# Moving 32 modulation slots from two feed-forward stages into two token mixers

## The chip, the cores and the metric

The kernel runs on one core of a Trainium2 chip. The metric is the device time of one launch in microseconds (us). Five engines work side by side, each through its own instructions in a fixed order: TensorE (PE, matmuls; PEld is its weight load), VectorE (DVE), ScalarE (ACT), GpSimd (POOL) and SyncE (SP, which here only issues DMAs). They wait for each other by semaphores.

## The reference, cut to what matters

Three transformer blocks run one after the other on 512 latent tokens (and 256 context tokens) of width 1024, all in float32. Each block starts from six modulation vectors per stream, computed from a conditioning vector alone, and not from the tokens:

```
m = jnp.dot(jax.nn.silu(cond), w_mod) + b_mod        # w_mod: 1024 x 6144
sh1, sc1, g1, sh2, sc2, g2 = split(m, 6)

h = rms_norm(x, norm1_g) * (1 + sc1) + sh1            # mixer
q, k, v, u_pool, a, b = split(h @ w_in)
attn = differential attention over latent and context tokens, 4 heads
mix  = concat(attn, pool_mixer(u_pool), conformer_conv(a, b))
x = x + g1 * (mix @ w_out)

h2 = rms_norm(x, norm2_g) * (1 + sc2) + sh2           # feed-forward (FFN)
x = x + g2 * ((silu(h2 @ w_g) * (h2 @ w_u)) @ w_down) # hidden width 2816
```

Blocks 0 and 1 have this form; in block 0 the context tokens go through the same steps. Block 2 has another mixer (latent attention and a gated recurrence) and the same kind of FFN. So the modulation of a block only has to be ready before that block uses it, and may be computed at any earlier time.

## The kernel before, in words

**Matmuls.** Weights and activations are split into a high and a low part (tiles `whi`/`wlo`, `hh`/`hl`, `gh`/`gl`), and every product is three matmuls (`mm3`, L255, L258, L259). A weight comes as two half tiles `raw` of 512 KB by SP's DMA queue (L227); ACT copies it to `whi` (L230), and POOL subtracts to get `wlo` (L231). Weights are loaded one ahead (`Weights.next`), `whi`/`wlo` have two buffers, and `raw` has four, taken in turn.

**Modulation slots.** The three blocks' modulation is cut into 72 slots of 256 columns (24 for each block). One slot, `mod_slot`, loads two `raw` halves (1 MB, L219, from the same four buffers and the same SP queue as the weights; the next slot's load is put in ahead of it), runs 8 small matmuls on PE (L344; the trace has two records of each), copies the result by ACT (`ev`, L350), transposes it with two PE matmuls (L355), and reduces, adds and scales on DVE (L357, L359, L363). The PSUM tiles of a slot carry a tag: `"pj"` in the mixers (the same two buffers that the projections of q, v and the pool use), `"ap"` in the FFNs, where no other matmul of that part uses it.

**Stages.** `start` runs 8 slots with the first norm. `layer(l)` is the mixer of block l: for each head there is a list of items (`windows`) that is issued step by step between the attention's steps. An item is a projection of the next head (`q`, `v`), four taps of the depthwise convolution (`t`; L666 on DVE, L671 on ACT, L672 on POOL), the pooling mixer, the convolution's layer norm, half of the output projection (`o`), or a modulation slot (`m`). `MODS_MIX[l]` gives the number of slots in the lists of heads 0 to 3. Attention runs at a raised priority, the taps at a lowered one. `ffn(l)` goes through 22 steps j of 128 hidden columns, with 48 matmuls on 512 latent columns each (and 48 on 256 context columns in block 0), and issues `MODS_FFN[l][j]` slots behind step j; after some steps a part of the down projection follows.

**Order.** The program's order is not the engines' order: a scheduler with its own estimate of durations and the priorities above sets, for each engine, what stands behind what. Once built, each engine's list is fixed, and an engine whose next instruction waits does nothing else.

Of the kernel before, what the change touches and what calls it, by code (L numbers as in the profile page):

```python
# [24 lines left out]
NJ = FF // 128  # L25
# [217 lines left out]
class K:  # L243
# [472 lines left out]
        return post(g, ps)  # L716


    MODS_MIX = [(4, 8, 0, 0), (2, 4, 2, 0)]
    MODS_FFN = [[1] * NJ, [1] * NJ, [0] * NJ]  # L720

    LAST = [(0, 0, 0.2, 0.4, 0.6, 0.8, 1), (0, 0.1, 0.4, 0.7, 1)]
    SLOT = {"g": 0, "u": 1, "p": 2, "v0": 3, "q0": 4, "q1": 5, "v1": 6, "q2": 7, "q3": 8}
# [1 line left out]
    def windows(self, l):  # L725
# [22 lines left out]
        q0, v0 = tm("q0"), tm("v0")  # L748
        nm = self.MODS_MIX[l]
        conv = [it for g in ("01", "2") for n in "gu" for it in fm(n) if it[2] in g]  # L750
# [175 lines left out]
    def ffn(self, l, pf, hx, hc, xt, xc, then, at=None):  # L926
# [5 lines left out]
        for gi, (j0, jn, cn) in enumerate(DOWN[l]):  # L932
            gt = []
            for j in range(j0, j0 + jn):
# [28 lines left out]
                gt.append((gh, gl))  # L963
                self.mod_fill(self.MODS_FFN[l][j], "ap", j == j0 + jn - 1)
                if at and j in at:
# [783 lines left out]
```

## Time and profile before

| | before |
|---|---|
| median of 3 runs | 2667.38 us (2660.89 to 2668.7) |
| profiled execution | 2666.06 us, of which the trace spans 2664.3 us |
| PE busy | 2516.9 us, 94% of the span |
| POOL, ACT, DVE busy | 1250.2, 959.7, 951.1 us |
| granted PE clock, mean | 0.966 |

The stages in the trace, read from where their tiles begin and end: start 0 to 104 us, mixer 0 from 104 (with its output projection to 479), FFN 0 from 479 to 1067, mixer 1 from 1067 to 1412 (its output projection from about 1349), FFN 1 from 1412 to 1827, block 2 from 1827 to the end. A row of a table of stretches gives each engine's busy time in it, the granted PE clock as a share of full speed, the DMA engines' busy share and GB/s. Busy time cannot tell a matmul at half clock from one at full clock, so both columns are read together.

### The profile page before, as it was taken

Reading aid. Unit: us, or ns where it says so; the run is one execution under the profiler, and the core shown is the slowest. Engines: PE = TensorE matmul, PEld = TensorE weight load, DVE = VectorE, ACT = ScalarE, POOL = GpSimd, SP = SyncE. Lnnn points to the kernel's source line nnn. Section 1 sums busy time; section 2 is a strip of 40 time slices with the busy share of each in tenths; the row PEclk is TensorE's granted clock in tenths of the full one; section 3 lists DMA queues with packets and bytes.
Section 4 is the critical chain, followed back from the end, with each engine's and each line's share of the span. In section 5 each row is a group of like instructions: output and inputs, shape, how many; then the busy total and the mean of one; then the engine's idle time right before and its main releaser. Section 6 shows DMA issues by size and latency. Waiting matters only on the chain.

```text
span 2664.3 us, 38718 instructions
## 1 busy us (share of the span) xinstructions
PE 2516.9 (94%) x15840; PEld 2143.2 (80%) x15840; DVE 951.1 (36%) x1864; ACT 959.7 (36%) x1973; POOL 1250.2 (47%) x1033
## 2 busy tenths in 40 slices
PE   7889979999999999999889999999998899999998
PEld 5767869988888889877788777778887788888887
DVE  4787463221120223479443111114321756210112
ACT  4454453412212123354434223224443543422222
POOL 4886323533333334688326445545322344555553
PEclk9889989999999999989989999999998899999999
DMA  7113311323223223222223434343101021223221
GB/s 251 48 48 96 127 71 33 111 85 121 87 94 104 95 96 100 78 64 80 90 85 115 162 121 161 123 154 115 64 32 50 16 87 56 80 95 95 94 89 55
DMA packets 68964, 248.57 MB, mean 93 GB/s; under 512 B 7473, under 2 KB 10801, under 8 KB 67121
## 3 DMA queue, kind: packets, MB, share of 16 engines
q1 hardware_dynamic: 64992, 231.11, 26.6%
q10 hardware_dynamic: 3792, 14.97, 1.5%
q8 instruction: 125, 2.05, 0.3%
q14 instruction: 55, 0.44, 0.1%
HBM read 239.75 MB, written 6.29 MB: 92 GB/s over the span
## 4 chain that ended last, share of the span: by engine, by line
PE 46%; DVE 6%; ACT 2%; POOL 2%; DMA 1%; issue 1%; POOLq 0%; DVEq 0%; ACTq 0%
PE s2t L259 6%; PE s2t L258 6%; PE s2t L255 6%; PE pj L255 5%; PE pj L258 5%; PE pj L259 5%; PE ap L829 1%; PE ap L258 1%; PE ap L259 1%; PE ap L255 1%; POOL wlo L231 1%; PE s2t L1535 1%; PE s2t L846 1%; DVE mix L666 1%; PE ap L344 1%
## 5 line engine op out<-in xcount | busy, mean ns | idle before, releaser
L231 POOL TENSOR_TENSOR wlo<-raw,whi 128x512 fp32r<-128x512 f32 x576 | 743.5, 1321 | 681.6 <-ACT whi L230 681.2
L230 ACT CAST whi<-raw 128x512 fp32r<-128x512 f32 x576 | 319.5, 616 | 670.0 <-PE pj L258 244.7
L255 PE MATMUL s2t<-hh,whi 128*128 128x512 f32 (+1 forms) x1184 | 445.8, 377 | 2.3 <-ACT whi L230 2.3
L259 PE MATMUL s2t<-hh,wlo 128*128 128x512 f32 (+1 forms) x1184 | 447.8, 378 | 0.0
L258 PE MATMUL s2t<-hl,whi 128*128 128x512 f32 (+1 forms) x1184 | 445.8, 377 | 0.8 <-POOL hl L429 0.8
L255 PE MATMUL pj<-hh,whi 128*128 128x256 f32 (+1 forms) x1088 | 336.8, 311 | 11.0 <-DVE mod L357 4.3
L258 PE MATMUL pj<-hl,whi 128*128 128x256 f32 (+1 forms) x1088 | 331.6, 305 | 2.1 <-POOL hl L429 1.1
L259 PE MATMUL pj<-hh,wlo 128*128 128x256 f32 (+1 forms) x1088 | 331.6, 306 | 0.3 <-POOL wlo L231 0.3
L959 DVE TENSOR_TENSOR sg<-sg,s2t 128x512 f32<-128x512 f32 x66 | 45.4, 688 | 652.9 <-ACT sg L958 652.9
L255 PEld LDWEIGHTS s2t<-hh,whi 128*128 128x128 f32 x1184 | 222.0, 188 | 48.3 <-ACT whi L230 3.0
L258 PEld LDWEIGHTS s2t<-hl,whi 128*128 128x128 f32 x1184 | 222.2, 188 | 46.7 <-POOL hl L429 1.5
L259 PEld LDWEIGHTS s2t<-hh,wlo 128*128 128x128 f32 x1184 | 222.5, 188 | 44.6 <-issue 1.2
L328 POOL TENSOR_TENSOR gl<-sg,gh 128x512 fp32r<-128x512 f32 (+1 forms) x66 | 97.5, 1478 | 289.1 <-ACT gh L327 289.0
L255 PEld LDWEIGHTS pj<-hh,whi 128*128 128x128 f32 x1088 | 210.0, 194 | 27.8 <-DVE mod L357 4.6
L258 PEld LDWEIGHTS pj<-hl,whi 128*128 128x128 f32 x1088 | 210.5, 193 | 11.4 <-POOL hl L429 1.4
L259 PEld LDWEIGHTS pj<-hh,wlo 128*128 128x128 f32 x1088 | 209.9, 193 | 8.8 <-POOL wlo L231 0.5
L255 PE MATMUL pj<-whi,hh 128*128 128x256 f32 x672 | 196.8, 293 | 0.9 <-ACT v L709 0.9
L258 PE MATMUL pj<-wlo,hh 128*128 128x256 f32 x672 | 196.2, 292 | 0.0
L259 PE MATMUL pj<-whi,hl 128*128 128x256 f32 x672 | 194.7, 290 | 0.0
L898 DVE SCALAR_TENSOR_TENSOR xt<-pj,mod,xt 128x256 f32<-128x256 f32 x224 | 101.7, 480 | 177.7 <-PE pj L259 176.6
L958 ACT ACTIVATE sg<-s2t 128x512 f32<-128x512 f32 x66 | 39.2, 594 | 303.8 <-PE s2t L259 303.8
L259 PE MATMUL pj<-gh,wlo 128*128 128x512 f32 (+1 forms) x400 | 146.1, 365 | 0.0
(388 smaller groups left out, 4759.9 us busy)
## 6 DMA issues: line engine op xcount, KB each, us to landing
raw<-in_w_mod SPq DMA_DIRECT2D x144, 512.0 KB, 4.0
raw<-in_w_up SPq DMA_DIRECT2D x132, 512.0 KB, 4.0
raw<-in_w_dn SPq DMA_DIRECT2D x66, 512.0 KB, 3.9
raw<-in_w_in SPq DMA_DIRECT2D x60, 512.0 KB, 3.9
raw<-in_w_out SPq DMA_DIRECT2D x24, 512.0 KB, 3.9
xt<-xs ACTq DMA_DIRECT2D x4, 1024.0 KB, 6.0
xt<-in_xT ACTq DMA_DIRECT2D x2, 1024.0 KB, 8.0
xs<-xt SPq DMA_DIRECT2D x2, 1024.0 KB, 3.9
```

The lines of the kernel that those rows point to most:

```text
L230: nc.scalar.copy(out=h, in_=raw[:, q])
L231: nc.gpsimd.tensor_tensor(out=lo[:, s][:, q], in0=raw[:, q], in1=h.bitcast(F32), op=ALU.subtract)
L255: i = mm(ps, lhsT=lh, rhs=rh, start=start, stop=False)
L258: mm(ps, lhsT=lh, rhs=rl, start=False, stop=False)
L259: return mm(ps, lhsT=ll, rhs=rh, start=False, stop=stop)
L328: (lo_eng or self.nc.vector).tensor_tensor(out=lo, in0=src, in1=hi.bitcast(F32), op=ALU.subtract)
L344: nc.tensor.matmul(ps[g:g + 32], lhsT=self.cond_t[:, k, :], rhs=raw[k // 4][:, k % 4, :], start=k < 4, stop=k >= 4, tile_position=(0, g))
L666: nc.vector.scalar_tensor_tensor(out=m, in0=u[:, j:j + W], scalar=dw(j), in1=m, op0=ALU.mult, op1=ALU.add)
L829: i = nc.tensor.matmul(o, lhsT=at[:, j], rhs=v[:, j0 + j, :], start=j0 + j == 0, stop=j0 + j == nj - 1)
L898: self.nc.vector.scalar_tensor_tensor(out=x, in0=ps, scalar=col, in1=x, op0=ALU.mult, op1=ALU.add)
L958: nc.scalar.activation(out=sg[:, c], in_=p[:, 0], func=AF.Silu)
L959: nc.vector.tensor_tensor(out=sg[:, c], in0=sg[:, c], in1=p[:, 1], op=ALU.mult)
```

## The change

Only two tables of numbers change. In the lists of the four heads of mixer 0 stand 8, 12, 6 and 4 slots (were 4, 8, 0, 0), in those of mixer 1 stand 6, 8, 6 and 2 (were 2, 4, 2, 0). FFN 0 issues a slot behind its first 8 steps (was all 22), FFN 1 behind its first 4 (was all 22). With the 8 of `start` there are 72 in both kernels, in the same order, with the same work in each.

```diff
-    MODS_MIX = [(4, 8, 0, 0), (2, 4, 2, 0)]
-    MODS_FFN = [[1] * NJ, [1] * NJ, [0] * NJ]
+    MODS_MIX = [(8, 12, 6, 4), (6, 8, 6, 2)]
+    MODS_FFN = [[1] * 8 + [0] * (NJ - 8), [1] * 4 + [0] * (NJ - 4), [0] * NJ]
```

The first place is PE's list at the end of the attention of mixer 0 (head 3, last steps): L650 is the pool's matmul, L829 and L825 the attention's product with v and its transposes, L344 and L355 a modulation slot, L255 to L259 on `hh` the output projection. Before:

```order
L650 MATMUL pj<-up_176,PW 128x256
L829 MATMUL ap<-v,at 128x128 x3
L825 MATMUL ap<-ident,e 128x128 x3
L650 MATMUL pj<-up_176,PW 128x512
L255 MATMUL pj<-hh,whi 128x256
L258 MATMUL pj<-hl,whi 128x256
L259 MATMUL pj<-hh,wlo 128x256
L255 MATMUL pj<-hh,whi 128x256
L829 MATMUL ap<-v,at 128x128 x3
```

And now:

```order
L829 MATMUL ap<-v,at 128x128 x3
L825 MATMUL ap<-ident,e 128x128 x3
L344 MATMUL pj<-raw,cond 32x256 x4
L355 MATMUL pj<-ident,ev 128x128 x2
L344 MATMUL pj<-raw,cond 32x256 x4
L829 MATMUL ap<-v,at 128x128 x3
L825 MATMUL ap<-ident,e 128x128 x3
L355 MATMUL pj<-ident,ev 128x128 x2
L344 MATMUL pj<-raw,cond 32x256 x8
L829 MATMUL ap<-v,at 128x128 x3
L355 MATMUL pj<-ident,ev 128x128 x2
L255 MATMUL pj<-hh,whi 128x256
```

Between the last attention steps stood output projections (132 of their 288 matmuls in mixer 0); now slots stand there, and 276 of the 288 come behind them.

The second place is SP's list of loads in mixer 0, where `in_w_in` and `in_w_out` are projection weights, `in_w_up` the FFN's, and `in_w_mod` the slots' halves. Before:

```order
L219 DMA raw<-in_w_mod 128x1024 x2
L227 DMA raw<-in_w_in 128x1024 x2
L219 DMA raw<-in_w_mod 128x1024 x6
L227 DMA raw<-in_w_in 128x1024 x2
L219 DMA raw<-in_w_mod 128x1024 x6
L227 DMA raw<-in_w_in 128x1024 x2
L219 DMA raw<-in_w_mod 128x1024 x10
L227 DMA raw<-in_w_out 128x1024 x5
L538 DMA nm<-in_rb 128x384
L552 DMA sq<-in_k_rope 128x512
L227 DMA raw<-in_w_out 128x1024 x3
L227 DMA raw<-in_w_up 128x1024 x4
```

And now:

```order
L227 DMA raw<-in_w_in 128x1024 x2
L219 DMA raw<-in_w_mod 128x1024 x12
L227 DMA raw<-in_w_in 128x1024 x2
L219 DMA raw<-in_w_mod 128x1024 x10
L227 DMA raw<-in_w_in 128x1024 x2
L219 DMA raw<-in_w_mod 128x1024 x14
L227 DMA raw<-in_w_out 128x1024 x2
L219 DMA raw<-in_w_mod 128x1024 x6
L538 DMA nm<-in_rb 128x384
L552 DMA sq<-in_k_rope 128x512
L219 DMA raw<-in_w_mod 128x1024 x14
L227 DMA raw<-in_w_out 128x1024 x6
```

Ten slots' loads now stand between the first slice of the output weight and the other three.

The third place is DVE's list in head 0 of mixer 0, around the first slot's reduction (L357) and its bias (L359), among the convolution's taps (L666), the softmax's maxima (L809) and the splits of q and k (L328). Before:

```order
L666 SCALAR_TENSOR_TENSOR mix_174<-uc,DWH,mix_174 128x783
L297 TENSOR_SCALAR rsv<-ss 128x8
L357 TENSOR_REDUCE mod_86<-pj 128x4
L328 TENSOR_TENSOR qk<-pj,qk 128x2x256
L809 TENSOR_REDUCE nmx<-s2t 128x1
L666 SCALAR_TENSOR_TENSOR mix_174<-uc,DWH,mix_174 128x783
L297 TENSOR_SCALAR rav<-ss 128x2
L359 TENSOR_TENSOR mod_86<-mod_86,PV 128x4
```

And now:

```order
L809 TENSOR_REDUCE nmx<-s2t 128x1
L666 SCALAR_TENSOR_TENSOR mix_174<-uc,DWH,mix_174 128x783
L357 TENSOR_REDUCE mod_86<-pj 128x4
L852 COPY r_1688<-rr 128x1
L853 SCALAR_TENSOR_TENSOR rr<-sa,lam_91,rr 128x1
L328 TENSOR_TENSOR qk<-pj,qk 128x2x256
L666 SCALAR_TENSOR_TENSOR mix_174<-uc,DWH,mix_174 128x783
L359 TENSOR_TENSOR mod_86<-mod_86,PV 128x4
```

The reduction stands earlier, with 7 taps of this pass still behind it, where 3 were behind it before.

## Rows read from the trace of the kernel before

**Rows 1.** The page's busy slices, 66.6 us each, in tenths; PEclk is the granted clock.

```profile
PE   7889979999999999999889999999998899999998
PEclk9889989999999999989989999999998899999999
```

**Rows 2.** Busy time by stage: stretch, its length, then each engine's busy us.

```profile
104.00:479.00 375.00, 332.43 (x2475) 294.16 (x2476) 232.64 (x460) 174.46 (x411) 202.63 (x154) 0.91 0.22 72
479.00:1067.00 588.00, 586.92 (x3733) 504.18 (x3732) 115.94 (x273) 140.38 (x271) 219.77 (x174) 1.00 0.30 100
1067.00:1349.00 282.00, 258.25 (x1851) 223.69 (x1850) 182.70 (x287) 137.65 (x300) 176.56 (x149) 0.92 0.23 74
1349.00:1412.00 63.00, 56.30 (x439) 54.68 (x439) 25.48 (x64) 20.76 (x50) 17.69 (x19) 0.95 0.24 84
1412.00:1827.00 415.00, 411.78 (x2247) 327.39 (x2246) 75.11 (x178) 135.83 (x267) 219.41 (x184) 1.00 0.44 143
```

**Rows 3.** ACT's timeline, first instruction behind each FFN step: FFN 1, then FFN 2.

```profile
1467.94 0.60 ACT L958 ACTIVATE sg<-s2t 128x512 f32<-128x512 f32 x1 [5.48 <-PE s2t L259]
1480.52 0.60 ACT L958 ACTIVATE sg<-s2t 128x512 f32<-128x512 f32 x1 [3.50 <-PE s2t L259]
...
2334.10 0.59 ACT L958 ACTIVATE sg<-s2t 128x512 f32<-128x512 f32 x1
2345.30 0.59 ACT L958 ACTIVATE sg<-s2t 128x512 f32<-128x512 f32 x1
```

**Rows 4.** The slots' matmuls alone (line 344) in FFN 1: PE, PEld.

```profile
1412.00:1827.00 415.00, 24.37 (x352) 9.21 (x352) 1.00 0.44 143
```

**Rows 5.** Busy time in parts of mixer 0, columns as in rows 2.

```profile
160.00:220.00 60.00, 46.17 (x304) 38.44 (x304) 44.62 (x56) 30.93 (x64) 50.09 (x29) 0.77 0.18 56
220.00:280.00 60.00, 55.85 (x457) 48.89 (x456) 49.19 (x121) 28.18 (x73) 37.21 (x32) 0.97 0.35 114
280.00:340.00 60.00, 58.19 (x493) 49.35 (x492) 29.73 (x77) 29.03 (x76) 19.11 (x17) 0.98 0.35 116
335.00:350.00 15.00, 7.00 (x33) 5.48 (x34) 9.41 (x19) 6.17 (x20) 10.43 (x8) 0.60 0.32 102
365.00:380.00 15.00, 11.17 (x67) 8.40 (x65) 14.25 (x36) 14.40 (x42) 2.43 (x1) 1.00 0.00 0
```

**Rows 6.** PE's timeline in mixer 0: start, us, instruction, and the idle before it.

```profile
183.18 0.58 PE L255 MATMUL pj<-hh,whi 128*128 128x256 f32 x1 [4.28 <-DVE mod L357]
183.55 0.41 PE L258 MATMUL pj<-hl,whi 128*128 128x256 f32 x1
183.77 0.41 PE L259 MATMUL pj<-hh,wlo 128*128 128x256 f32 x1
...
188.69 0.28 PE L258 MATMUL pj<-hl,whi 128*128 128x256 f32 x1
188.81 0.28 PE L259 MATMUL pj<-hh,wlo 128*128 128x256 f32 x1
```

**Rows 7.** PE's waits in mixer 0 to 380 us: us in total, times, longest.

```profile
PE ap L875 <- DVE on L872: 13.7, 4, 5.7
PE pj L255 <- DVE mod L357: 4.3, 1, 4.3
```

**Rows 8.** DMA issues from 270 to 310 us: count, KB each, median us to landing.

```profile
raw<-in_w_mod SPq DMA_DIRECT2D x10, 512.0 KB, 4.4
```

**Rows 9.** DVE's timeline before the reduction of that slot, columns as in rows 6.

```profile
181.81 1.23 DVE L297 TENSOR_SCALAR rsv<-ss 128x8 f32<-128x8 f32 x1
182.96 0.16 DVE L357 TENSOR_REDUCE mod<-pj 128x4 f32<-128x16 f32 x1
```

**Rows 10.** SP's waits in mixer 0, columns as in rows 7.

```profile
SPq L219 <- PE pj L344: 60.4, 9, 14.3
```

**Rows 11.** What PE stood idle for before line 344 in mixer 0: us, times.

```profile
  issue: 1.9, 8
```

**Rows 12.** PE's waits in mixer 1's output projection, 1349 to 1412 us.

```profile
PE s L255 <- ACT whi L230: 4.1, 1, 4.1
```

## The prediction

> **What bounds the kernel now.** I read the page's slices first: PE is at 9 tenths nearly everywhere, and where it dips the granted clock dips too [rows 1]. Then the table by stage [rows 2], which tells two kinds of stage apart. In FFN 0 and FFN 1 PE is busy for 586.92 of 588 us and 411.78 of 415 us at clock 1.00; there each PE instruction taken away is time. The mixers are not full: mixer 0 with its output projection has PE busy for 332.43 of 375 us at clock 0.91, mixer 1 for 258.25 of 282 and 56.30 of 63 us at 0.92 and 0.95. That is 42.6 us idle in mixer 0 and 23.8 + 6.7 = 30.5 us in mixer 1. The lower clock takes 375 x 0.09 = 34 us in the one and 282 x 0.08 + 63 x 0.05 = 26 us in the other. So the mixers have some 130 us in which PE, by its own speed, could have done more. Why they have it is in PE's waits [rows 7] and its timeline [rows 6]: PE follows a fixed list, and stops when DVE, ACT or POOL has not finished what the next matmul needs. It is not fed too slowly by weights there: the waits for DVE lead.
>
> **What a slot costs in an FFN.** FFN 1 has a slot behind every step, FFN 2 has none, and both have the same 48 matmuls on 512 columns for a step. The step takes 1480.52 - 1467.94 = 12.58 us with a slot and 2345.30 - 2334.10 = 11.20 us without [rows 3]: 1.38 us a slot. The slot's matmuls are 24.37 / 22 = 1.11 us of it [rows 4], and the rest is the two transposes. FFN 0 runs the same instructions at the same clock [rows 2], so I take the same price there. FFN 0 loses 22 - 8 = 14 slots, 14 x 1.38 = 19.3 us; FFN 1 loses 18, 24.8 us. Together -44.1 us. Nothing is late next: FFN 2 runs its steps at exactly the matmuls' pace without slots [rows 3], so weights, casts and POOL's subtraction keep up at 11.2 us a step, and FFN 0's steps are longer. The copy and the DVE reductions of these slots hid behind PE before, and their going is worth nothing. I take this term as sure to some 3 us.
>
> **What the same slots cost in the mixers.** Mixer 0 gets 18 more, mixer 1 gets 14 more. The cost is not in the trace, so I bound it. Below: all goes into idle time, 0, and if the filled gaps also bring back a third of the 60 us that the clock takes, -20. Above: nothing is hidden, 32 x 1.38 = 44 us, and two waits grow. The first is the PSUM buffer: with tag "pj" a slot holds a buffer that the projections need, until DVE has reduced it. One of the 12 slots of mixer 0 made PE stand for 4.28 us that way (start 183.18 us) [rows 6, 7], 4.3 / 12 = 0.36 us a slot, so 11.5 us for 32. The second is the load: a slot's halves take the raw buffers of the slot two before it, and land 4.4 us after their issue [rows 8]. In the new PE list I count eight slots, six in mixer 0, that have under 30 matmuls between them and the slot two before. At 0.12 us for 256 columns (188.69 to 188.81) [rows 6], some 24 matmuls last 2.9 us, and 1.5 us of the landing is not covered: 8 x 1.5 = 12 us. So the bounds are -20 and 44 + 11.5 + 12 = +68 us.
>
> Between these I choose by place. Of the 18 in mixer 0, about three stand before the point that the old trace reached at 220 us; from 160 to 220 us PE was idle for 13.8 us at clock 0.77 [rows 5], and I count them as free. Five fall where 220 to 340 us was: 114.0 of 120 us busy at 0.97 and 0.98 [rows 5], and I count them in full, 5 x 1.38 = 6.9 us. Ten stand at the end of the attention. There PE was idle for 8.0 of 15 us (335 to 350) and 3.8 of 15 (365 to 380) [rows 5], but the slots also take the place of 120 matmuls of the output projection (120 x 0.12 = 14.4 us, about their own length) that filled the last steps and now come behind. I count these ten at half, 6.9 us. For mixer 1, with 30.5 us idle spread over it [rows 2], I count half of 14 x 1.38, 9.7 us. Of the two waits I take 3 us: the buffer's was one case in twelve, and in the new DVE list the first reduction stands earlier.
>
> Sum: -44.1 + 6.9 + 6.9 + 9.7 + 3 = -17.6 us. The profiled execution took 2666.06 us (span 2664.3 and 1.8 around it), 1.3 under the median of the three runs, so I predict 2667.4 - 17.6, about 2650 us.
>
> **A rule that speaks against it.** The reduction for which PE waits until 183.18 us lasts 0.16 us, and stood behind the convolution's taps and an operation of 1.23 us [rows 6, 9]. Were it so for one slot in three, the waits would be 11 x 4.3 = 47 us instead of my 3, and the change would lose 26 us. I give this little weight: in the new DVE list 7 taps are left behind the first reduction, and most of the added slots come after the taps. The Trainium skill, "TensorE: Matmul & The Clock Gate", Part 1 (the HAM clock gate), has it that the queues of VectorE and ScalarE are strictly first in, first out; the trace agrees here, in that the reduction starts only when the 1.23 us operation is over.
>
> **The rivals.** (a) The mixers absorb all. For it: 73 us idle in them against 44 us of slots [rows 2]. Against it: the ten at the end replace other filler. It gives -44 us, 2623. With the clock: in mixer 0 a 256-column matmul goes every 0.21 us (183.55 to 183.77) after the 4.28 us stop, and every 0.12 us five microseconds on [rows 6]. This is the step from 1.2 to 2.4 GHz; filled stops would spare it, down to 2605. The same page of the Trainium skill, in the same part, has it that the low clock is the default and that activity lifts it; by this the filled mixers would go faster, and the trace's clock of 0.60 beside 8 us idle (335 to 350) agrees [rows 5].
>
> (b) Work is only moved: the engines' lists stay as badly fitted as before, the stops stay, and each slot costs its 1.38 us in the mixers too. For it: PE's largest wait there, 13.7 us for DVE's normalisation of the attention [rows 7], has nothing to do with slots, and a stop is filled only if a slot happens to stand just before it in the list. Net 0, 2667.
>
> (c) Slower: the raw ring. SP already waited 60.4 us, nine times, for a slot's matmuls to free a buffer [rows 10]. Ten slots' loads now stand ahead of the second to fourth slices of the output weight, so these can start only when PE has passed the last slots. Load, cast and subtraction follow, and the output projection starts late; in mixer 1 a late weight at that place cost 4.1 us [rows 12]. With the eight tight slots at the whole landing time of 4.4 us (35 us), 2 x 4.1 us for the weights, and the slots hidden to the half I forecast, the mixers cost 23.5 + 35 + 8 = 67 us against 44: +22, about 2690. It decides from the point where waits in the mixers exceed 20 us. Against it: SP's waits were hidden so far; before the slots' own matmuls in mixer 0 PE stood for 1.9 us in all, and not for a DMA [rows 11].
>
> **Chances.** Forecast (mixers absorb about half) 0.52; (a) 0.14; (b) 0.20; (c) 0.14. I take 0.3%, 8 us, as what can be told from no change: 2659 to 2675. Faster: 0.14 + 0.52 less a tail of 0.06, plus 0.03 from (b), 0.63. Same: 0.14 of (b), the 0.06, and 0.02 of (c), 0.22. Slower: 0.15. The likeliest case alone spans 2636 to 2662; to leave out no more than two in ten the range goes into (a) and (c), 2622 to 2684.
>
> **What would show it.** In the new profile the FFN steps without a slot are 11.2 us apart in FFN 1, and FFN 0 and 1 are shorter by 19 and 25 us. If they are not, the first term is wrong. Mixers 0 and 1 together last some 26 us longer, with less idle and an equal or higher clock; at 0 it is (a), at 44 it is (b). PE waits for raw at line 344, or for whi at the first output projection, mean (c); waits for mod at line 357 mean the rule above. The prediction fails if the two mixers grow by over 36 us or under 10.

## The result, and the profile after

The changed kernel takes 2692.16 us (median of 4 runs, 2689.39 to 2698.4), the kernel before 2667.93 us beside it: ratio 1.0098, 95% interval 1.0081 to 1.0115. It is 26 us slower by the ratio, which all changes below go by (24 by the medians), and 42 above the forecast. The profiled execution of the changed kernel took 2698.4 us (span 2696.6), 6 above its median, so differences read from it are a few us too large. Over runs of one kernel the time goes with the granted clock: beside the last two experiments the kernel before took 2653.76 us at a mean clock of 0.972 and 2668.08 us at 0.965.

The page's slices [rows 1] look the same; the slots did not fill the dips:

```profile
PE   7898988999999999997989999999998898999998
PEclk9888998999999999988989999999999899999999
```

The FFNs together gave what was forecast. First and last instruction behind an FFN step (ACT, line 958: duration ns, then first and last start), FFN 0 and FFN 1, of the kernel before:

```profile
L958 ACT ACTIVATE sg<-s2t x22: 587/599/600, 493.6 to 1026.8; 128x512 f32<-128x512 f32 x22
L958 ACT ACTIVATE sg<-s2t x22: 588/598/602, 1439.8 to 1801.9; 128x512 f32<-128x512 f32 x22
```

And of the changed kernel:

```profile
L958 ACT ACTIVATE sg<-s2t x22: 586/589/597, 537.7 to 1055.1; 128x512 f32<-128x512 f32 x22
L958 ACT ACTIVATE sg<-s2t x22: 584/584/601, 1498.7 to 1834.3; 128x512 f32<-128x512 f32 x22
```

FFN 0 went from 533.2 to 517.4 us and FFN 1 from 362.1 to 335.6, together -42.3 (forecast 19.3 and 24.8 less). A step of FFN 1 without a slot takes what FFN 2's took [rows 3]:

```profile
1541.28 0.58 ACT L958 ACTIVATE sg<-s2t 128x512 f32<-128x512 f32 x1
1552.48 0.58 ACT L958 ACTIVATE sg<-s2t 128x512 f32<-128x512 f32 x1
```

The loss is in the mixers. By these marks mixer 0 (from 104 us to the first FFN step) went from 389.6 to 433.7 us, mixer 1 (last step of FFN 0 to the first of FFN 1) from 413.0 to 443.6: +74.7 in these two executions, +68 by the ratio (26 + 42), where I forecast +26.5. Of mixer 0's 44.1 us, 2.2 belong to the start: its last transposes (line 801) begin at 105.25 instead of 103.02 us. Block 2 did not change (862.4 and 862.3). The mixers' stages again [rows 2], cut where they now begin and end:

```profile
104.00:524.00 420.00, 378.22 (x2807) 314.68 (x2808) 232.59 (x504) 183.47 (x434) 207.47 (x156) 0.90 0.33 110
1094.00:1396.00 302.00, 273.14 (x2063) 229.11 (x2061) 181.66 (x310) 135.69 (x298) 172.61 (x146) 0.91 0.33 108
1396.00:1472.00 76.00, 64.98 (x500) 61.07 (x500) 30.01 (x76) 28.33 (x70) 24.21 (x24) 0.91 0.33 111
```

Mixer 0 has 42 us of idle PE and a clock of 0.90, as before; in mixer 1 the idle time even grew, 28.9 + 11.0 us against 30.5. So in the sum the slots' work came on top of the idle time. Between the marks (mixer 0, then mixer 1), before:

```profile
104.00:493.60 389.60, 347.03 (x2603) 308.05 (x2604) 238.68 (x473) 181.72 (x428) 207.96 (x160) 0.91 0.23 75
1026.80:1439.80 413.00, 381.14 (x2854) 341.44 (x2850) 239.54 (x419) 197.93 (x442) 239.95 (x215) 0.94 0.25 83
```

And after:

```profile
104.00:537.70 433.70, 391.92 (x2928) 327.66 (x2929) 238.53 (x516) 189.79 (x449) 211.34 (x161) 0.91 0.33 111
1055.10:1498.70 443.60, 399.97 (x3071) 348.28 (x3070) 240.43 (x446) 199.13 (x452) 238.64 (x214) 0.92 0.32 108
```

PE's busy time grew by 44.9 and 18.8 us, its idle time by -0.8 and +11.8. PE's largest wait in the whole of mixer 0 was, before (us in all, times, longest; [rows 7] go to 380 us only):

```profile
PE ap L875 <- DVE on L872: 17.8, 5, 5.7
```

And in the changed kernel PE waited there, among others, for these:

```profile
PE pj L255 <- ACT whi L230: 7.0, 2, 5.5
PE ap L875 <- DVE on L872: 5.7, 4, 2.9
PE pj L344 <- DMA raw<-in_w_mod: 3.9, 4, 1.7
```

And in mixer 1 with its output projection (1094 to 1472):

```profile
PE pj L801 <- POOL y L792: 6.3, 4, 2.6
PE pj L344 <- DVE mod L357: 5.4, 1, 5.4
PE pj L255 <- ACT whi L230: 4.6, 1, 4.6
PE ap L875 <- DVE on L872: 4.5, 2, 3.8
PE pj L801 <- DVE mod L357: 3.9, 2, 3.6
```

The wait for the attention's normalisation shrank in mixer 0, 17.8 to 5.7 us: a slot stands right ahead of six of its twelve places now, where none did, so some slots did fill idle time. In its place came waits that were small or absent before: the second to fourth slices of the output weights (`whi` at L255), the slots' landings (`raw`), their reductions (`mod`). SP's queue shows why the weights are late: 14 halves of slots now stand ahead of them there, and take 47 us to issue, since they wait for raw buffers (start, length):

```profile
367.31 47.07 SPq L219 DMA_DIRECT2D raw<-in_w_mod  x14
417.47 12.52 SPq L227 DMA_DIRECT2D raw<-in_w_out  x3
```

And PE's timeline there, with the idle time ahead of an instruction in brackets:

```profile
421.22 0.44 PE L875 MATMUL ap<-ident,on 128*128 128x128 f32 x2 [0.54 <-DVE on L872]
427.12 0.58 PE L255 MATMUL pj<-hh,whi 128*128 128x256 f32 x1 [5.46 <-ACT whi L230]
...
434.57 0.41 PE L259 MATMUL pj<-hh,wlo 128*128 128x256 f32 x1
434.79 0.41 PE L255 MATMUL pj<-hh,whi 128*128 128x256 f32 x1
```

Behind the stop the starts are 0.22 us apart instead of 0.12: the clock has fallen to its lower level.

The slots' own rows in mixer 0 (matmuls and transposes; us, mean ns, idle ahead), before:

```profile
L344 PE MATMUL pj<-raw,cond 128*32 128x256 f32 x192 | 14.1, 406 | 0.0
L355 PE MATMUL pj<-ident,ev 128*128 128x128 f32 x24 | 5.3, 297 | 0.3 <-DVE qk L328 0.3
```

After, 29.0 us more for 18 slots:

```profile
L344 PE MATMUL pj<-raw,cond 128*32 128x256 f32 x480 | 35.2, 409 | 4.9 <-DMA raw<-in_w_mod 3.9 <-ACT up L604 0.7
L355 PE MATMUL pj<-ident,ev 128*128 128x128 f32 x60 | 13.2, 305 | 1.0 <-DVE qk L328 1.0
```

One more line grew that has nothing to do with slots, the attention's scores (line 846, matmuls on 64 rows, issued in pairs). In mixer 0, before:

```profile
L846 PE MATMUL s2t<-qk 64*128 64x512 f32 x96 | 32.2, 440 | 0.0
L846 PE MATMUL s2t<-qk 64*128 64x256 f32 x144 | 31.8, 316 | 4.3 <-DVE qk L328 3.6 <-ACT qk L327 0.7
```

After:

```profile
L846 PE MATMUL s2t<-qk 64*128 64x512 f32 x96 | 37.1, 459 | 1.4 <-ACT e L813 1.4
L846 PE MATMUL s2t<-qk 64*128 64x256 f32 x144 | 36.1, 333 | 1.7 <-ACT e L813 1.0 <-ACT qk L327 0.7
```

The same 240 matmuls take 9.2 us more. In PE's list of mixer 0 they stand in 73 groups, 35 of them of one matmul (before 51 and 8): the scheduler has put projection matmuls between the halves of pairs. In mixer 1 it is otherwise: single ones rose from 13 to 19, and the same lines became shorter by 5.9 us. The larger of the two there, before and after:

```profile
L846 PE MATMUL s2t<-qk 64*128 64x512 f32 x96 | 36.5, 483 | 4.0 <-ACT e L813 3.7 <-ACT qk L327 0.3
...
L846 PE MATMUL s2t<-qk 64*128 64x512 f32 x96 | 31.7, 467 | 2.0 <-ACT e L813 2.0
```

### The profile page after: what moved, and what is told of

Same layout as the page of the kernel before. It is cut to its first block, busy times and chain, and to the rows that moved or that the text cites. A ratio compares the mean times of both kernels' runs of the same rounds, so it can differ in the third digit from the quotient of the medians.

```text
span 2696.6 us, 38771 instructions
## 1 busy us (share of the span) xinstructions
PE 2536.8 (94%) x15840; PEld 2153.8 (80%) x15840; DVE 934.3 (35%) x1864; ACT 952.2 (35%) x1973; POOL 1249.8 (46%) x1033
## 4 chain that ended last, share of the span: by engine, by line
PE 46%; DVE 6%; ACT 2%; POOL 2%; issue 1%; DMA 1%; POOLq 0%; DVEq 0%; ACTq 0%
PE s2t L255 6%; PE s2t L258 6%; PE s2t L259 6%; PE pj L255 5%; PE pj L258 5%; PE pj L259 5%; PE ap L829 2%; PE ap L255 1%; PE ap L258 1%; PE ap L259 1%; DVE mix L666 1%; PE s2t L1535 1%; POOL wlo L231 1%; PE s2t L846 1%; PE ap L825 1%
## 5 line engine op out<-in xcount | busy, mean ns | idle before, releaser
L255 PE MATMUL s2t<-hh,whi 128*128 128x512 f32 (+1 forms) x1184 | 447.8, 379 | 0.0
L259 PE MATMUL s2t<-hh,wlo 128*128 128x512 f32 (+1 forms) x1184 | 445.9, 377 | 0.0
L255 PE MATMUL pj<-hh,whi 128*128 128x256 f32 (+1 forms) x1088 | 337.2, 311 | 17.7 <-ACT whi L230 11.6
L259 PE MATMUL pj<-hh,wlo 128*128 128x256 f32 (+1 forms) x1088 | 332.7, 307 | 0.6 <-POOL wlo L231 0.3
L259 PEld LDWEIGHTS s2t<-hh,wlo 128*128 128x128 f32 x1184 | 222.7, 188 | 46.9 <-issue 0.8
L255 PEld LDWEIGHTS s2t<-hh,whi 128*128 128x128 f32 x1184 | 222.4, 188 | 44.6 <-issue 1.2
L255 PEld LDWEIGHTS pj<-hh,whi 128*128 128x128 f32 x1088 | 211.3, 195 | 34.7 <-ACT whi L230 12.6
L259 PEld LDWEIGHTS pj<-hh,wlo 128*128 128x128 f32 x1088 | 211.1, 194 | 9.6 <-POOL wlo L231 1.4
L255 PE MATMUL pj<-whi,hh 128*128 128x256 f32 x672 | 201.4, 300 | 5.2 <-DVE qk L328 3.6
L259 PE MATMUL pj<-whi,hl 128*128 128x256 f32 x672 | 198.2, 295 | 0.0
L255 PE MATMUL pj<-gh,whi 128*128 128x512 f32 (+1 forms) x400 | 145.8, 366 | 0.0
L259 PE MATMUL pj<-gh,wlo 128*128 128x512 f32 (+1 forms) x400 | 145.6, 364 | 0.0
L258 PE MATMUL pj<-gl,whi 128*128 128x512 f32 (+1 forms) x400 | 145.4, 364 | 0.0
## 6 DMA issues: line engine op xcount, KB each, us to landing
xt<-in_xT ACTq DMA_DIRECT2D x2, 1024.0 KB, 13.8
```

Of the source, the lines that this page charges most:

```text
L255: i = mm(ps, lhsT=lh, rhs=rh, start=start, stop=False)
L258: mm(ps, lhsT=lh, rhs=rl, start=False, stop=False)
L259: return mm(ps, lhsT=ll, rhs=rh, start=False, stop=stop)
```

## The experiments

The theories at the start: **A**, the slots disturb the attention (split score pairs, late weights); **C**, nothing hides a slot's PE time; **E**, the raw ring and the late output weights. Changes in us are the ratio's, on 2665.

**One mixer at a time.** Only mixer 0's part (against the changed kernel):

```diff
-    MODS_MIX = [(8, 12, 6, 4), (6, 8, 6, 2)]
-    MODS_FFN = [[1] * 8 + [0] * (NJ - 8), [1] * 4 + [0] * (NJ - 4), [0] * NJ]
+    MODS_MIX = [(8, 12, 6, 4), (2, 4, 2, 0)]
+    MODS_FFN = [[1] * 4 + [0] * (NJ - 4), [1] * NJ, [0] * NJ]
```

> Only the first mixer's part of the change: 30 slots in mixer 0 and 4 in FFN 0, mixer 1 and FFN 1 as before (8 and 22). By the trace of the changed kernel the 18 added slots cost mixer 0 44.1 us and take 15.8 to 25 out of FFN 0. Theory A (the slots disturb the attention of mixer 0: score pairs split, clock lowered; output weights late): +19 to +28, 2687 to 2696 us. Rival B (the cost is the late output weights, 7.0 us in mixer 0 and 4.6 in mixer 1, and the rest is spread evenly over 32 slots): +9 to +12 here, about 2678.

And only mixer 1's, `[(4, 8, 0, 0), (6, 8, 6, 2)]` with FFN 0 full and 8 slots in FFN 1:

> Only the second mixer's part: 22 slots in mixer 1 and 8 in FFN 1, mixer 0 and FFN 0 as before (12 and 22). Theory A: mixer 1 +30.6 for 14 slots against 14 x 1.47 = 20.6 out of FFN 1: +10, 2678 us. Rival B (even over the slots): 14 of 32 of +24, +10 as well; together with the run of mixer 0's part the two must make +24 if nothing is shared between the mixers.

Measured 1.0049 (1.0031 to 1.0067), +13, and 1.0045 (1.0031 to 1.0059), +12. The two add up to the whole, 25 of 26; neither mixer is the culprit, and A's +19 to +28 for the first was too much; B's +9 to +12 is within the interval. PE's order in mixer 0 is word for word that of the changed kernel, yet mixer 0 took 422.4 us here and 433.7 there: one execution's stage is good to some 11 us, so I go by the ratios from here on.

**Score matmuls first**, in the changed kernel and in the one before:

```diff
+                        with self.tc.high_priority(100000):
                             nc.tensor.matmul(s[c][:, k0:k1], lhsT=qk[r, 0, a, t], rhs=qk[r, 1, b, k0:k1], start=n == 0, stop=n == 2)
```

> The changed kernel with each score matmul put ahead of all that is ready when the order is made, so that the two matmuls of a pair (64 rows each) stand together on the PE. In mixer 0 single ones go from 35 of 73 groups to 3 of 48. Theory A (split pairs and the clock that falls behind them): the 10.6 us that the scores gained in PE time go, and some of the clock loss: 2668 to 2682 us. Rival C (the slots are simply not hidden, 2.3 us each): no change, 2690 to 2695. Rival D (scores first holds up the projections and the output transposes that the next head needs): slower than 2695.

> The kernel before with the same edit of the score matmuls alone. There 8 of 51 groups in mixer 0 and 13 of 41 in mixer 1 stand singly. Theory A: 21 singles fewer at about 0.3 us a switch, -3 to -6 us: 2661 to 2665. Rival C: no change. Rival D: slower.

Measured 1.0077 (1.0054 to 1.0100), +20.5, and 0.9994 (0.9977 to 1.0010). About 6 us of the loss go, by itself no more than the intervals allow; in the kernel before nothing does. A part at most.

**The output weights.** Their loads ahead of the last slots:

```diff
                         early.close()
                         then()
+                        ws["o"] = self.out_weights(l, 0)
                         return lambda: None
...
-                        if name not in ws:
-                            ws[name] = self.out_weights(l, 0, 1)
+                        if len(ws[name]) == 1:
+                            ws[name] += self.out_weights(l, 1)
```

> The changed kernel with the loads of the output weights issued ahead of the last list's slots (4 in mixer 0, 2 in mixer 1), so that those weights don't stand behind them in the raw buffers. Theory E (late output weights: 7.0 us of PE's wait in mixer 0 and 4.6 in mixer 1, and a lower clock behind them): 9 to 14 us of the loss go, 2675 to 2683 us if the kernel before stands at 2664. Theory C (the slots cost their own PE time because nothing hides them): within 4 us of the changed kernel's 2690.

The last slots among the output projections:

```diff
-            [("sp", int(g), 0) for g in gr] + [("x",)] + mod(nm[3])
-            + merge([("o", int(g), m) for g in gr for m in range(KD)], [("sp", int(g), 1) for g in gr]),
+            [("sp", int(g), 0) for g in gr] + [("x",)]
+            + merge([("o", int(g), m) for g in gr for m in range(KD)], [("sp", int(g), 1) for g in gr], mod(nm[3])),
```

> The changed kernel with the last list's slots (4 and 2) spread among the output projections instead of standing ahead of them. Theory E: as in the run with the output weights' loads first, 2675 to 2683 us. Theory C: no change, about 2690, since the slots only move. Rival F (the slots now stand in the stretch where PE has no idle time and stretch the projections): 2692 or more.

Measured 1.0057 (1.0041 to 1.0074), +15, and 1.0058 (1.0037 to 1.0079), +15.5: 11 us of the loss either way, as theory E had it. In both, PE waits nowhere for `whi` at a `pj` matmul of L255. The late weights are shown; that they are 11 of the 26 is good to some 6 us in each run.

**Slots with a part left out.** No loads (a resident tile of constants in their place):

> The changed kernel, but the 52 slots of the two mixers read a resident tile of constants: their 104 loads of 0.5 MB each are left out, and with them every place that they take in the raw buffers. Matmuls, transposes, ACT and DVE parts stay. Theory E (raw ring and late weights): most of the 26 us goes, 2664 to 2675 us. Theory C (PE time): 2682 to 2690, only PE's waits for landings (4.6 us) and a part of the late weights (up to 11.6) go.

No PE work:

> The changed kernel, but the matmuls and transposes of the 52 slots in the mixers are left out; ACT copies its part from the loaded slices and DVE reduces that. Loads, ACT and DVE work and their order stay. Theory C (52 slots cost their PE time of some 1.6 us, nothing hidden): 52 x 1.4 to 1.6 = 73 to 83 us less than the changed kernel, 2607 to 2617. Theory G (a part was hidden: the 20 slots that stood in the mixers before cost nothing): 32 x 1.4 to 1.6 = 45 to 51 less, about 2640. Theory E: no more than 30 less, 2660.

No ACT, DVE and transposes:

> The changed kernel, but of the 52 slots in the mixers only the loads and the eight matmuls are left; the transposes and ACT's and DVE's parts are left out. Theory H (a slot's copy on ACT and reduction on DVE stand in the queues of the softmax, and wait there for their matmuls: DVE idle ahead of the reductions rose from 6.2 to 21.6 us in mixer 1): most of the loss that is not the late output weights goes, and the 20 old slots gain as well: 2635 to 2660 us. Theory C (PE time): only the transposes go (0.44 us a slot, 52 of them, 23 us): about 2668. Theory E alone (loads): no change, 2690.

And no slot at all in the mixers, with places and clock kept:

```diff
                     if name == "m":
-                        return self.mod_slot(*self.mods.pop(0))
+                        self.mods.pop(0)
+                        return lambda: None
```

> The changed kernel with the 52 slots of the mixers left out entirely; their places in the lists and their step of the recording clock stay. By theories C, E and H what goes is all that 52 slots cost in the mixers: 72 to 75 for the 32 added ones by the profile of the changed kernel and 0 to 45 for the 20 old ones: 2575 to 2620 us. Theory I (the order in which everything else is recorded is shifted by the slots' places, and that costs): above 2630.

Measured: no loads 1.0044 (1.0026 to 1.0061), +12, so loads cost 14, little more than the late weights. No PE work 1.0024 (1.0007 to 1.0040), +6: only 20 us less than the changed kernel, where C had said 73 to 83. No ACT, DVE and transposes 1.0017 (1.0000 to 1.0035), +4.5. No slots 0.9919 (0.9892 to 0.9946), -22: 48 us less for 52 slots. The third came out as C had it, but the second and the fourth fell so far short that C seemed ruled out. It was not: PE's largest wait, over the whole trace, without any slots is

```profile
PE ap L875 <- DVE on L872: 57.3, 10, 11.3
```

against 20.5 us before. What was taken out left holes, since all else kept the order that was made around the slots.

**Fewer, and later.** The opposite change, no slot in mixer 1, `[(4, 8, 0, 0), (0, 0, 0, 0)]`, FFN 0 with 30 slots:

> The opposite change to the kernel before: no slot in mixer 1 (before 8), the 8 of them in FFN 0, which issues 30 instead of 22; mixer 0 keeps 12, FFN 1 22. FFN 0 grows by 8 x 1.15 to 1.38 = 9 to 11 us. If a slot in the second mixer costs more than in an FFN from the first one on (as 33 us for 14 slots), mixer 1 gives back 8 x 2.0 to 2.4 = 16 to 19 and the kernel is faster, 2653 to 2658. If the first 8 slots are hidden there and only those above cost, mixer 1 gives nothing back: 2672 to 2675.

And the slots' parts recorded later:

```diff
-        return [(0, post), (1, post2)]
+        return [(0, post), (1, post2)] if tag == "ap" else [(1, post), (4, post2)]
```

> The changed kernel with each slot's ACT copy recorded 1 us and its transposes and DVE reduction 4 us later in the mixers, so that they stand behind more of the softmax's work and find their matmuls done. Theory H: 10 to 20 us of the loss go, 2670 to 2680. Rival J (the two PSUM buffers that the slots share with the projections are held longer): slower than the changed kernel, above 2695. Theory C: no change, about 2690.

Measured 1.0002 (0.9987 to 1.0018): a slot costs in mixer 1, on the average of its first eight, about the 1.3 us that it adds in FFN 0 (543.5 us there, by 8 slots more than 533.2); both readings of the expectation miss. And 1.0137 (1.0102 to 1.0173), +36.5: theory H falls, and J has the time, but not by what it named: PE's waits for the slots' copies and reductions are 12.8 us in that run against 13.8 in the changed kernel. So nothing shows the reductions in the softmax's queue to be what costs.

**Places.** The slots' items shift a head's list against the attention's steps. First without slots, places and clock step:

> As the run without any slots in the mixers (the 52 slots left out), but their places in the lists and the step of the recording clock go too: everything else is recorded as if there had never been slots. Theory I (the shifted order costs): well below the 2641 us of the run with places, 2595 to 2625. Theory L (the attention's chain bounds a mixer without slots): 2636 to 2646, as with places.

Then the changed kernel with a list cut by its other items, without the clock's step, and the kernel before cut in the same way:

```diff
-                    n = int(len(win[hd + 1]) * share[hd + 1][t] + 0.01)
+                    n = self.cut(win[hd + 1], share[hd + 1][t])
...
+    def cut(self, items, share):
+        left = int(sum(it[0] != "m" for it in items) * share + 0.01)
+        n = 0
+        while n < len(items) and (left > 0 or (n and items[n][0] == "m")):
+            left -= items[n][0] != "m"
+            n += 1
+        return n
```

> The changed kernel with all its slots, but a head's list is cut into the attention's steps by its other items alone: each projection, tap and norm is recorded in the step in which it stands without slots, and the slots beside it. The clock's step per slot stays. Theory I with the places as its cause: most of the 15 us that are not late weights go, and 2670 to 2680 us. Theory L and theory C: no change, 2688 to 2694.

> The changed kernel without the 1 us that each slot in the mixers adds to the recording clock; places as in the change. The stages that wait for the clock (the turns of q and k, the norms, the pooling's weights) are then recorded after as much other work as without slots. Theory I with the clock as its cause: 2670 to 2680 us. Theory L and theory C: no change, 2688 to 2694; a loss if the slots' own copies and reductions, recorded later by this, hold the PSUM buffers longer (as the run with the parts later, 2697).

> The kernel before with the lists cut by the other items alone, its 20 slots in the mixers as they were. Theory I with the places as its cause: a gain of 3 to 15 us, 2650 to 2662. Theory L: no change, 2665.

Without slots and places 0.9777 (0.9758 to 0.9797), -59: the shifted order alone costs 37 us when no slot fills its holes. PE's same wait is down to

```profile
PE ap L875 <- DVE on L872: 24.7, 9, 6.5
```

With the slots in them the holes are no loss: places kept 1.0076 (1.0059 to 1.0093), +20; no clock step 1.0089 (1.0074 to 1.0104), +24; and the kernel before gets slower by it, 1.0026 (1.0013 to 1.0039). So theory I holds for a kernel without slots, and is worth some 6 us of ours, near the limit of what can be told. What the run without slots gives is a floor: of its -59, 42 are the FFNs', so the 20 slots of before cost some 17 us in the mixers, 0.9 each, so a part of theirs was hidden, against 2.1 for each of the 32 added. Mixers 0 and 1 there:

```profile
104.00:482.60 378.60, 337.19 (x2384) 303.12 (x2385) 240.23 (x444) 177.29 (x415) 207.85 (x159) 0.91 0.13 44
1000.20:1405.80 405.60, 365.75 (x2675) 334.15 (x2674) 232.93 (x394) 188.55 (x426) 237.82 (x214) 0.94 0.18 61
```

In mixer 0 PE idles for 41.4 us with no slots, 42.6 with 12, 41.8 with 30. That the three agree does not mean that slots reach none of it: with the same 30 slots and the output weights' loads ahead of the last ones it is 28.3 us:

```profile
104.00:517.70 413.70, 385.38 (x2924) 323.47 (x2925) 237.39 (x512) 187.77 (x445) 206.30 (x159) 0.92 0.34 116
```

In the changed kernel new waits took the place of those that the slots had filled.

**The cross-check.** The three remedies together, in the changed kernel:

> The changed kernel with the output weights' loads ahead of the last slots, the places kept and the score matmuls first. Apart these took 11, 6 and 6 us off its loss of 26. If they are separate terms: 26 - 23 = +3, 2665 to 2671 us: what stays is that 32 slots cost about what the FFNs gain. If they are one disturbance seen three ways: 2676 to 2682, as the best of them alone.

And pure PE work added to the kernel before, the slots' eight matmuls twice:

```diff
-        for k in range(KD):
+        for k in [*range(KD)] * (2 if tag == "pj" else 1):
             g = 32 * (k % 4)
```

> The kernel before with the eight matmuls of each of its 20 mixer slots issued twice in a row: 20 x 1.17 to 1.5 us = 23 to 30 us more work on PE, with no load, no ACT or DVE part, no place and no buffer added. Theory C (nothing hides PE work in the mixers): +20 to +30, 2685 to 2695 us. Theory of the prediction (half of it falls into PE's 75 us of idle time): +10 to +15, 2675 to 2680. If PE's idle time takes it all: no change, 2665, and the loss of the change lies in what comes with the slots, not in their PE work.

The remedies: 0.9985 (0.9969 to 1.0002), -4, within no change from before: 30 us of the changed kernel are gone, no less than the 23 that the three took apart, so they act on separate terms. Mixers 0 and 1 of that run, 9.8 and 21.7 us longer than before:

```profile
104.00:503.40 399.40, 365.46 (x2928) 312.21 (x2928) 239.66 (x514) 187.94 (x446) 206.06 (x160) 0.96 0.35 121
1020.80:1455.50 434.70, 390.65 (x3071) 345.79 (x3070) 241.76 (x446) 200.47 (x452) 236.94 (x214) 0.94 0.32 110
```

The three together were not tried in the kernel before. Apart, scores first changed nothing there and places kept cost 7 us; the loads were not tried.

The doubled matmuls: 1.0122 (1.0088 to 1.0157), +32.5, for 23.2 us of added work, which the slots' own rows show. Mixer 0, then mixer 1 of that kernel (lines 14.1 and 11.0 before):

```profile
L344 PE MATMUL pj<-raw,cond 128*32 128x256 f32 x384 | 30.4, 412 | 2.5 <-ACT sq L770 2.0 <-DVE mod L357 0.5
...
L344 PE MATMUL pj<-raw,cond 128*32 128x256 f32 x256 | 17.9, 384 | 0.0
```

As a sum nothing hid it. With no item moved, the scheduler made 35 single scores of mixer 0's 240 here too, and their lines grew by the same 9 us as in the changed kernel:

```profile
L846 PE MATMUL s2t<-qk 64*128 64x512 f32 x96 | 37.0, 462 | 2.8 <-ACT qk L327 2.8
L846 PE MATMUL s2t<-qk 64*128 64x256 f32 x144 | 36.1, 334 | 6.8 <-DVE qk L328 5.5 <-ACT qk L327 0.7 <-ACT e L813 0.7
```

In mixer 1, with 25 single ones (before 13), they became shorter by 5.9 us, as in the changed kernel. So the number of single scores alone does not give their cost.

## Why the prediction was wrong, point by point

1. **The FFNs' gain** (-44.1): right in the sum, -42.3. By luck in part: one price for both was wrong, as FFN 0 gave 1.13 us a slot (15.8 for 14) and FFN 1 1.47 (26.5 for 18), against 1.38.
2. **Half of the slots' time hides in the mixers** (6.9 + 6.9 + 9.7 for 32 slots): this step failed: the mixers grew by 68 us, where I had set 36 as the mark of failing. I took PE's idle time as room, and what the slots bring with them as 3 us. The idle time is made of waits at fixed places of PE's list; in mixer 0 slots did fill some of the attention's (17.8 to 5.7 us), but new waits came in their place. The slots' matmuls and transposes grew by 29.0 us in mixer 0 and 22.6 in mixer 1 (lines 344 and 355, tag "pj"; 1.61 us a slot), and the idle time changed by -0.8 and +11.8. With the three disturbances put right, 32 slots cost 42 - 4 = 38 us in the mixers (34 to 43 by the interval), 1.2 each, against 1.32 saved in the FFNs: by my price of 1.38 about a seventh of it hidden, where I had counted on nearly half. Single executions suggest that the two mixers differ: in the run with the remedies the 18 slots of mixer 0 cost 9.8 us, some half hidden, and the 14 of mixer 1 21.7, nothing hidden. As executions differ by as much, this stays open. Rival (b) came nearest, that each slot costs its price in the mixers as well.
3. **The two waits cost 3 us**: mis-sized. The buffer wait (PE for `mod`) is 11.2 us against 4.3, the landings are 4.6 instead of none, and the late output weights, which I named only under rival (c), are 11 us by two runs.
4. **Not in the sum at all**: that more work in a head's list makes the scheduler reorder what is already there. Split score pairs and shifted places go with the rest of the 30 us, 19 together; how they share it is not settled, since each alone is about as large as its interval. That the pairs are a term is argued from mixer 0; mixer 1's scores became faster.
5. **Rival (c)** gave the right time, 2690, half for the wrong reason: the late weights came (11.6 us of waits, forecast 8.2), the landings cost 4.6 us and not 35, and the slots were not half hidden. **The rule weighed** stays minor: taking the reductions out of the queues along with the transposes gained what the transposes and little else would, and putting them later lost 10 us. The reduction of [rows 9] starts at 182.96 us, 0.08 before the operation ahead of it ends: in order, but not only when that is over.
6. **The bound**: +68 by the ratio is the upper end that I had worked out, and then given almost no weight. That it fits is luck: I had 44 + 11.5 for the buffer + 12 for the landings, the runs give 38 + 11 for the late weights + 19.

So the account of the loss: -42 in the FFNs; +38 for the slots' work; +30 for what it upset, of which 11 are the late weights. The 38 is what the three remedies leave, and holds so far as these would have given the kernel before nothing.

## What to carry to other kernels

Idle time of an in-order engine is room only for work that stands just ahead of the wait; before counting on it, find the place in the engine's list, and otherwise price moved work in full. A filled wait is no gain yet if the work's loads and buffers bring new ones. Where a scheduler makes the list, price what it will do to the work that was there, first of all loads that share a ring. And leaving work out is a fair test only if the rest gets the order that it would have had without it: here the same 52 slots were worth 48 us by the one test and 85 by the other.

## What the runs showed of the hardware that was not expected

A matmul on 64 rows that alternates with one on 128 rows costs both their overlap. In the changed kernel six score matmuls in a row take 0.56 us (123.91 to 124.47), but alternating with a projection each start comes 0.31 us after the other, where projections follow each other by 0.12:

```profile
123.91 0.62 PE L846 MATMUL s2t<-qk 64*128 64x256 f32 x6
124.47 0.44 PE L825 MATMUL ap<-ident,e 128*128 128x128 f32 x2
...
141.30 0.38 PE L846 MATMUL s2t<-qk 64*128 64x256 f32 x1
141.62 0.39 PE L255 MATMUL pj<-whi,hh 128*128 128x256 f32 x1
141.93 0.38 PE L846 MATMUL s2t<-qk 64*128 64x256 f32 x1
142.24 0.38 PE L258 MATMUL pj<-wlo,hh 128*128 128x256 f32 x1
```

The Trainium skill, "TensorEngine Tiling (Array Packing)", Key Properties, says that changing the tiling mode drains the engine; by these rows a switch costs some 0.2 us.

And the granted clock can fall while the profile, which models the ends of matmuls, shows no idle time of PE. Right behind these rows:

```profile
140.00:145.00 5.00, 5.00 (x23) 3.20 (x21) 0.00 (x0) 4.39 (x8) 4.92 (x5) 0.99 0.01 2
145.00:150.00 5.00, 5.00 (x11) 2.75 (x11) 1.31 (x2) 0.38 (x1) 4.12 (x3) 0.50 0.60 187
150.00:155.00 5.00, 5.00 (x25) 5.00 (x25) 1.99 (x6) 2.79 (x7) 0.69 (x1) 0.50 0.06 23
```

It fell from 2.4 to 1.2 GHz with PE busy in every row. In the run of mixer 0's part alone, with the same order of PE's instructions, it fell at the same place (0.50 from 143.4 to 150.2 us, PE busy for all 6.80). That the alternation brought it down is argued, not shown: no run tried it alone.
